# A first tap behind a copy on ScalarE, and block sums emitted over two plain tiles, in a two-layer encoder

## The chip, the cores and the metric

The kernel runs on one core of one Trainium2 chip. The metric is the time on the device in microseconds, the median of several runs. The core has five engines, each with a queue of instructions: TensorE (PE) multiplies matrices and writes into the banks of PSUM; VectorE (DVE) and ScalarE (ACT) do elementwise work; GpSimd (POOL) and SyncE (SP) mostly issue DMA transfers here. Engines wait for one another through semaphores.

## The reference

Two layers over 512 tokens of 1024 features, all in float32. Layer 0 mixes with an mLSTM and a memory attention, layer 1 with a band attention and a memory attention. After each mixer comes the same channel mixer, the part that the change is in:

```python
def conv_ffn(h, w_up, conv_w, conv_b, w_down):
    u, g = jnp.split(h @ w_up, 2, axis=-1)
    g = causal_dwconv(g, conv_w, conv_b)
    return (jax.nn.silu(g) * u) @ w_down
...
    x = x + jnp.concatenate([mix_out, mem_out], axis=-1) @ w_out
    x = x + conv_ffn(rmsnorm(x, norm_ffn_g[l]), ffn_w_up[l], ffn_conv_w[l], ffn_conv_b[l], ffn_w_down[l])
```

The hidden width is 2816, that is 22 tiles of 128 channels, each with an "up" and a "gate" half. The convolution has three taps along the tokens: y[t] = w2 g[t] + w1 g[t-1] + w0 g[t-2] + b.

## The kernel before

**Layout and precision.** Activations lie with the features on the 128 partitions and the 512 tokens along the free dimension: `xT` is 8 tiles of 128 x 512. A float32 operand is split into a high part (a cast, ScalarE, L142) and a low part (what is left, VectorE, L143), and `mm3` (L194 to L198) replaces one product by three matmuls: high x high, high x low, low x high. So every operand of a product costs one ScalarE and one VectorE instruction first. `scaled` (L329) does the same for an x tile times its norm gain (L331, L332).

**Stages of a layer.** Mixer; then `OutProjection.finish` (L710), which for each of the 8 x tiles takes the output projection's result (the last three x tiles, j = 5 to 7, are projected right there, 24 matmuls each), adds it to `xT[j]` (L715), sends `xT[j]` to DRAM, adds its square to the norm's sum (L290, L291) and makes the scaled high and low parts; then `channel_mixer` (L1014).

**The channel mixer.** The first three of the 22 tiles are *plain* (`PLAIN` = 3, `plain`, L759): gate and up are each a chain of 8 x 3 matmuls of 512 columns, then taps, Silu, products (L770 to L778) and the split of the result. The other 19 go through `step` (L874) with seven half-size products instead of eight. For that the x tiles are combined: `block_sums` (L781) is a generator; each of its four turns k takes x tiles k and k + 4, scales both on ScalarE (L787), forms four differences of 128 x 256 on VectorE (L796) and splits them (four casts on ScalarE, four low parts on VectorE). The weights are combined likewise by `Forms` (L916), one step ahead.

**One step.** TensorE runs seven chains of 12 matmuls of 256 columns. The first goes into bank r1, the second into r2; the third, fifth and sixth again into r1, the fourth and seventh into r3. Between the fifth and the sixth, and between the sixth and the seventh, stand chains of the down projection for tiles finished earlier: their number and length per step are given by `LOADS` and `UNITS` (L44 to L47), so that some steps have twice as much of it as others, and the last has none. ScalarE copies r1 out after the first chain (L890) and, through `sum_products` (L882), after the third, fifth and sixth; each next chain into r1 waits for the copy before it. VectorE adds r2 (L893).

**The tail.** What remains of a tile is done in the next step by a `Tail` (L980): `last_block` (L988, VectorE adds r3), `scaled` (L991, VectorE: gate times the norm row), `scaled_up` (L994, the same for up), `first_tap` (L996: on ScalarE, scale and bias, L750, and it prepares the other two taps), `second_tap` and `third_tap` (L743, VectorE; after the third ScalarE's Silu, L1006), `gated` (L1009), `split`. The first step of a layer has no tail. `split_fourth` (L970) splits the step's fourth weight sum: cast on ScalarE, low part on VectorE. `add_down` copies a down chain's result (L822) and adds it to x in DRAM with an accumulating DMA from the POOL queue (L823); the copies rotate through the `bias` buffers, four of them, of which the second layer holds two for the final gain.

**What sets the order.** Inside `later` (L850) a `manual_schedule` covers PE, ScalarE and VectorE: there each engine's queue is exactly the order in which the code emits. Everywhere else a planner orders each engine's queue by its own costs and due times: what is emitted earlier goes first, but an instruction whose inputs and buffers it takes to be ready may be put into a gap ahead of others. `weave(job, filler, each)` (L227) emits job and after each of its yields adds `each` to a counter; whenever that reaches 1, it emits one turn of the filler. The block sums are such a filler: one turn after each of the x tiles 4, 5 and 6 in `finish` (L719), the fourth turn in the first plain tile (five yields at 0.25).

**Buffers.** Split parts and block sums share the tag `u` (50 buffers of 128 x 512), temporaries the tag `t` (8), weights three pairs `wh`, `wl`, the step's weight halves `fh`, `fl` (4 each). PSUM: tag `mm` 3 banks, `sc` 3, `tr` 2.

Of the kernel before, what the change touches and what calls it, by code (L numbers as in the profile page):

```python
# [19 lines left out]
KT = D // P  # L20
# [36 lines left out]
def trunk(  # L57
# [34 lines left out]
    def sb(tag, shape, dtype=F32):  # L92
        count[0] += 1
        return pool.tile(shape, dtype, tag=tag, name=f"{tag}{count[0]}", bufs=bufs[tag])

    def ps(tag):
        count[0] += 1
        return psum.tile([P, S], F32, tag=tag, name=f"p{tag}{count[0]}", bufs=pbufs[tag])
# [101 lines left out]
    def project(w, c0, act, tag="mm"):  # L200


        n = len(act)
        wh, wl = weights(rows(w, c0, P), n, P)
        o = ps(tag)
        for k in range(n):
            mm3(o, wh[:, k, :], wl[:, k, :], act[k][0], act[k][1], k == 0, k == n - 1)
            yield
        return o

    def run(gen):
        while True:
            try:
                next(gen)
            except StopIteration as end:
                return end.value

    def chain(*gens):
        for g in gens:
            yield from g  # L220
# [6 lines left out]
    def weave(job, filler, each, lead=0):  # L227

        due = lead
        for n in chain([0], job):  # L230
            due += each if n is None else each * n
            while due >= 1:
                due -= 1
                next(filler, None)
# [39 lines left out]
    def logarithms():  # L274

        pin(A.preload_act_table_set("natural_log_exp_and_others"))

    class Norm:
# [14 lines left out]
        def finish(self):  # L293


            parts = [sb("t", [P, S], F32R) for _ in range(2)]
            split(*parts, self.acc)
            yield 7.4
            o = ps("sc")
            for i, part in enumerate(parts):  # L300
                nc.tensor.matmul(o, onesr, part, start=i == 0, stop=i == 1)
            v, r, t = sb("rb", [P, S]), sb("t", [P, S]), sb("t", [P, S])
            A.activation(t, o, AF.Ln, scale=1.0 / D, bias=eps)
            V.tensor_scalar(v, o, 1.0 / D, EPS, op0=ALU.mult, op1=ALU.add)
            A.activation(r, t, AF.Exp, scale=-0.5)
            A.activation(t, r, AF.Square)
            yield 4
            V.scalar_tensor_tensor(t, t, -0.5, v, op0=ALU.mult, op1=ALU.mult)
            self.row = sb("rb", [P, S])
            V.scalar_tensor_tensor(self.row, t, 1.5, r, op0=ALU.add, op1=ALU.mult)  # L310
# [18 lines left out]
    def scaled(t, g):  # L329
        hi, lo = sb("u", [P, S], F32R), sb("u", [P, S], F32R)  # L330
        A.activation(hi, t, AF.Copy, scale=g)  # L331
        V.scalar_tensor_tensor(lo, t, g, f(hi), op0=ALU.mult, op1=ALU.subtract)  # L332
        return hi, lo
# [121 lines left out]
    def reload_x():  # L455
        for j in range(KT):
            xT[j] = sb("fh" if j < KT // 2 else "fl", [P, S])
            tc.keep_in_program_order(nc.sync.dma_start(xT[j], xspill[j]))
# [6 lines left out]
    with tc.manual_schedule(engines={mybir.EngineType.PE, mybir.EngineType.Activation, mybir.EngineType.DVE}):  # L465
# [20 lines left out]
        def step(products, os_, k, order):  # L486
            for a, b in order:
                for i, o in enumerate(os_):
                    c = slice(i * P, (i + 1) * P)
                    st, mv = kv[k][a], memT[k][b]  # L490
                    first, last = (k, (a, b)) == (0, order[0]), (k, (a, b)) == (KT - 1, order[-1])
                    if products == "keys":
                        nc.tensor.matmul(o, st[:, c], mv, start=first, stop=last)
                    else:
                        nc.tensor.matmul(o, mv[:, c], st[:, MEM:], start=first, stop=last)
# [26 lines left out]
        for q in range(KT // 2):  # L522
            k = 2 * q
            step("keys", ko, k, weights_last if q else ((0, 0), (1, 0), (0, 1)))
            if not q:
                step("values", vo, k, weights_last)
            if q < KT // 2 - 1:
                split(*parts_of[q + 1], memory_rows(q + 1, ("tr", "sc")[q % 2], range(2)))
                for j in (k + 2, k + 3):
                    split(*kv[j], kvraw[j])  # L530
            if q:
                step("values", vo, k, weights_last)
            step("keys", ko, k + 1, weights_last)
            if q == KT // 2 - 1:
                kws1 = [parts(kraw1[0], block=0)]
                keep(0, 0, ko)
                kws1.append(parts(kraw1[1], block=1))
            step("values", vo, k + 1, weights_last)
# [151 lines left out]
    class OutProjection:  # L690
# [19 lines left out]
        def finish(self, mixer):  # L710
            logarithms()
            norm = mixer.norm
            for j in range(KT):
                o = self.o[j] if j in self.o else run(project(self.w, j * P, self.mixes))
                V.tensor_add(xT[j], xT[j], o)  # L715
                pin(G.dma_start(xspill[j], xT[j]))
                norm.add(xT[j])
                mixer.act.append(scaled(xT[j], mixer.gain[:, j : j + 1]))
                if KT // 2 <= j < KT - 1:  # L719
                    next(mixer.forms)  # L720

    class ChannelMixer:
# [151 lines left out]
        def step(self, j, w, nxt, tail):  # L874
            def then(o, *names):
                for name in names if o is not None else ():
                    getattr(o, name)()

            def sum_products(o, r, w, i):

                self.products(r, w, self.t(i))
                A.copy(o, r[:, :H])  # L882

            new = Tail(self, j)
            then(tail, "last_block", "scaled", "first_tap", "scaled_up")
            w.split_fourth()
            r1, r2, new.r3 = ps("mm"), ps("mm"), ps("sc")
            new.up, new.u3, new.pre = sb("t", [P, S]), sb("t", [P, S]), sb("t", [P, S])
            self.products(r1, w.a11, self.b(0, 0), True)
            A.copy(new.up[:, :H], r1[:, :H])  # L890
            then(tail, "second_tap", "third_tap")
            self.products(r2, w.a12, self.b(1, 0), True)
            V.tensor_tensor(out=new.up[:, :H], in0=new.up[:, :H], in1=r2[:, :H], op=ALU.add)  # L893
            sum_products(new.up[:, H:], r1, w.s2, 2)
            then(nxt, "sums")
            self.products(new.r3, w.s1, self.t(1), True)
            then(tail, "gated")
            then(nxt, "split_second", "sum_third")
            sum_products(new.u3[:, :H], r1, w.s3, 3)
            then(tail, "split")  # L900
            then(nxt, "split_up")
            V.tensor_tensor(out=new.pre[:, H:], in0=new.u3[:, :H], in1=new.r3[:, :H], op=ALU.add)
            w.down_products(0, 2)
            then(nxt, "split_sums", "sum_fourth")
            w.add_down(0)
            then(nxt, "split_gate")
            w.add_down(1)
            then(nxt, "split_down")
            sum_products(new.pre[:, :H], r1, w.a22, 4)
            w.down_products(2, 4)  # L910
            self.products(new.r3, w.s4, self.b(1, 1))
            w.add_down(2)
            w.add_down(3)
            return new, nxt
# [98 lines left out]

    def channel_mixer(mixer):  # L1014

        weave(mixer.plain(0), mixer.forms, 0.25)
        run(mixer.forms)
        mixer.buffers()
        skips = -(turn[0] + 2 * (PLAIN - 1)) % 3
        for j in range(1, PLAIN):  # L1020
            turn[0] += j <= skips
            run(mixer.plain(j))
        mixer.later()
        reload_x()
        return mixer.hid[FT - LAST :]
# [296 lines left out]
    mixer = ChannelMixer(0, col["gffn"][:, 0:8], more_rows)  # L1322
    outp.finish(mixer)
    hid = channel_mixer(mixer)
    logarithms()
    norm2, kvact, act = Norm(), [], []
# [134 lines left out]
    mixer = ChannelMixer(1, col["gffn"][:, 8:16], lambda: None)  # L1461
# [28 lines left out]
    def final_norm(T):  # L1490
# [8 lines left out]
        for c in range(0, S, step):  # L1499
# [5 lines left out]
            if last:  # L1505
                nc.scalar.dma_start(out[T * P : (T + 1) * P, :S], xt[T][0])

    hid = channel_mixer(mixer)
    n = LAST // 2
    for hf in range(2):  # L1510
# [76 lines left out]
```

## Time and profile before

| | |
|---|---|
| time, median of 3 runs | 1212.64 us (1211.23 to 1212.66) |
| the profiled execution's own time | 1212.91 us |
| its span, first to last instruction | 1211.2 us |
| mean granted TensorE clock | 0.997 |
| busy: VectorE, ScalarE | 986.1 us (81%), 741.4 us (61%) |
| HBM traffic over the span | 137 GB/s |

In the profile, a row of the timeline gives start and duration in us, engine, line of the kernel, operation, output and inputs, and in brackets the engine's idle time ahead of the instruction and what ended it. L142 and L143 are lines of a helper, so the tile names tell what is split: `fh`, `fl` a step's second, fourth or sixth weights, `wh`, `wl` other weights, `u` activations. A matmul that is shown with 0.28 us is pipelined: the next may start 0.11 us after it. The windows view gives the busy time of each engine in a stretch, the granted clock, and the DMA engines' share.

In the timeline the first layer's channel mixer covers about 280 to 597 us, the second's about 846 to 1166 us. The 38 copies at L890 lie between 310.6 and 1159.5 us.

### The profile page before, as it was taken

The numbers are of one execution on the slowest core, as the hardware profiler recorded it, in microseconds if no ns is written. First come the engines' busy times: TensorE is split into PE (matmuls) and PEld (weight loads), VectorE is DVE, ScalarE is ACT, GpSimd is POOL, SyncE is SP. The second block draws the span as 40 slices with busy tenths as digits, with TensorE's granted clock in tenths as the row PEclk, the third lists the DMA queues.
The fourth block names the chain that finished last, engine by engine and source line by source line (L and its number), as shares of the span: only waits on it lengthen the run. The fifth ranks groups of instructions, "written<-read, shape, count | busy, mean of one in ns | idle before, by whom it ended". The sixth has DMA issues, their size and how long they took to land.

```text
span 1211.2 us, 19132 instructions
## 1 busy us (share of the span) xinstructions
PE 1183.3 (98%) x7149; PEld 1044.9 (86%) x7149; DVE 986.1 (81%) x1768; ACT 741.4 (61%) x1345; POOL 143.1 (12%) x238
## 2 busy tenths in 40 slices
PE   9999999999999999999999999998998999999997
PEld 9988888887898899999888888787788889999986
DVE  6786788789789888888788888988977988888864
ACT  6448586667566555555566666767654655555545
POOL 1111101010122111011020001101011111011100
PEclk9999999999999999999999999999999999999999
DMA  8645324344677766655673323235447665656551
GB/s 286 213 108 140 80 76 128 92 147 116 150 164 155 164 161 161 140 139 114 175 216 85 89 60 125 77 105 163 133 99 139 131 140 139 140 139 140 122 156 70
DMA packets 200623, 162.87 MB, mean 134 GB/s; under 512 B 8680, under 2 KB 176334, under 8 KB 200530
## 3 DMA queue, kind: packets, MB, share of 16 engines
q1 hardware_dynamic: 182066, 119.74, 33.6%
q0 software_dynamic: 17888, 40.86, 18.0%
q8 instruction: 56, 0.92, 0.3%
q10 hardware_dynamic: 576, 1.05, 0.2%
q14 instruction: 37, 0.30, 0.1%
HBM read 128.89 MB, written 36.66 MB: 137 GB/s over the span
## 4 chain that ended last, share of the span: by engine, by line
PE 74%; issue 14%; DVE 6%; ACT 4%; DMA 2%; POOL 1%; POOLq 0%; SPq 0%; ACTq 0%; DVEq 0%
PE pmm L196 15%; PE pmm L197 14%; PE pmm L198 14%; PE ptr L197 5%; PE ptr L198 5%; PE ptr L196 5%; PE psc L198 4%; PE psc L197 4%; PE psc L196 3%; PE psc L602 2%; DVE wl L143 1%; ACT wh L142 1%; DMA wr<-in_a_w_in_dram 1%; ACT t L750 1%; PE ptr L1409 1%
## 5 line engine op out<-in xcount | busy, mean ns | idle before, releaser
L196 PE MATMUL pmm<-u,wh 128*128 128x512 f32 (+1 forms) x984 | 336.6, 342 | 0.2 <-ACT u L142 0.2
L198 PE MATMUL pmm<-u,wl 128*128 128x512 f32 (+1 forms) x984 | 332.1, 338 | 3.4 <-DVE wl L143 3.4
L197 PE MATMUL pmm<-u,wh 128*128 128x512 f32 (+1 forms) x984 | 332.2, 338 | 0.7 <-DVE u L332 0.7
L143 DVE TENSOR_TENSOR wl<-wr,wh 128x1024 fp32r<-128x1024 f32 (+4 forms) x172 | 195.4, 1137 | 82.2 <-ACT wh L142 81.7
L142 ACT CAST wh<-wr 128x1024 fp32r<-128x1024 f32 (+4 forms) x172 | 168.3, 981 | 83.3 <-PE pmm L197 33.2
L198 PEld LDWEIGHTS pmm<-u,wl 128*128 128x128 f32 x984 | 184.8, 188 | 23.3 <-DVE wl L143 4.0
L196 PEld LDWEIGHTS pmm<-u,wh 128*128 128x128 f32 x984 | 184.9, 188 | 18.6 <-ACT u L142 1.0
L197 PEld LDWEIGHTS pmm<-u,wh 128*128 128x128 f32 x984 | 185.0, 188 | 18.2 <-DVE u L332 1.4
L823 POOL DMA_DIRECT2D xspill<-bias x80 | 69.3, 874 | 445.2 <-ACT bias L822 417.9
L143 DVE TENSOR_TENSOR fl<-pt,fh 128x512 fp32r<-128x512 f32 x114 | 78.5, 689 | 36.7 <-ACT fh L142 33.8
L196 PE MATMUL ptr<-u,wh 128*128 128x512 f32 x272 | 106.4, 391 | 0.0
L197 PE MATMUL ptr<-u,wh 128*128 128x512 f32 x272 | 106.4, 391 | 0.0
L198 PE MATMUL ptr<-u,wl 128*128 128x512 f32 x272 | 106.0, 390 | 0.0
L196 PE MATMUL pmm<-u,fh 128*128 128x256 f32 x304 | 89.3, 294 | 13.6 <-ACT t L890 13.0
L142 ACT CAST fh<-pt 128x512 fp32r<-128x512 f32 x114 | 70.1, 617 | 26.2 <-DVE pt L939 26.0
L197 PE MATMUL pmm<-u,fh 128*128 128x256 f32 x304 | 85.3, 281 | 0.0
L198 PE MATMUL pmm<-u,fl 128*128 128x256 f32 x304 | 84.9, 279 | 0.0
L750 ACT ACTIVATE t<-t,cols 128x512 f32<-128x512 f32 x44 | 35.9, 816 | 71.3 <-DVE t L991 69.3
L196 PEld LDWEIGHTS pmm<-u,fh 128*128 128x128 f32 x304 | 57.6, 189 | 23.0 <-ACT t L890 20.9
L822 ACT COPY bias<-ptr 128x512 f32<-128x512 f32 x80 | 46.9, 589 | 41.1 <-PE ptr L198 35.5
L1006 ACT ACTIVATE t<-t 128x512 f32<-128x512 f32 x38 | 24.1, 633 | 74.9 <-DVE t L743 74.9
L198 PE MATMUL psc<-u,wl 128*128 128x256 f32 (+1 forms) x216 | 67.4, 312 | 0.4 <-DVE wl L143 0.4
(348 smaller groups left out, 2663.2 us busy)
## 6 DMA issues: line engine op xcount, KB each, us to landing
wr<-in_ffn_w_up_dram SPq DMA_DIRECT2D x50, 512.0 KB, 7.1
xspill<-bias POOLq DMA_DIRECT2D x80, 256.0 KB, 5.7
pt<-in_ffn_w_up_dram SPq DMA_DIRECT2D x38, 512.0 KB, 8.0
wr<-in_ffn_w_down_dram SPq DMA_DIRECT2D x34, 512.0 KB, 5.2
wr<-in_a_w_in_dram SPq DMA_DIRECT2D x20, 512.0 KB, 3.9
wr<-in_w_kv_dram SPq DMA_DIRECT2D x12, 512.0 KB, 3.9
xspill<-fh POOLq DMA_DIRECT2D x16, 256.0 KB, 2.6
xspill<-fl POOLq DMA_DIRECT2D x16, 256.0 KB, 2.5
```

Of the source, the lines that this page charges most:

```text
L142: high = A.copy(hi, src) if on_act else V.tensor_copy(hi, src)
L143: low = V.tensor_tensor(out=lo, in0=src, in1=f(hi), op=ALU.subtract)
L196: nc.tensor.matmul(o, lh, rh, start=first, stop=False, skip_group_check=more)
L197: nc.tensor.matmul(o, lh, rl, start=False, stop=False, skip_group_check=more)
L198: nc.tensor.matmul(o, ll, rh, start=False, stop=last, skip_group_check=more)
L602: nc.tensor.matmul(o, a, b, start=first and i == 0, stop=i == 1)
L750: A.activation(acc, src, AF.Identity, scale=self.fw[:, 2 * FT + j : 2 * FT + j + 1], bias=self.fb[:, j : j + 1])
L822: A.copy(t, o)
L823: G.dma_start(xspill[j], t, accum_op=ALU.add)
L1006: A.activation(self.acc, self.acc, AF.Silu)
L1409: nc.tensor.transpose(tp[:, b * P : (b + 1) * P], es[T, h][:, b * P : (b + 1) * P], ident)
```

## The change

Three edits:

- `OutProjection.finish` emits turns of the block sums only in layer 0. In layer 1 it emits none.
- `channel_mixer` weaves the block sums through all three plain tiles at 0.125 a yield, and emits what is left of them after the last plain tile instead of after the first. The first plain tile has five yields left after the norm, so no turn falls to it; each of the two others has 16 yields, so a turn follows its 8th yield (the end of its gate chain) and one its 16th (the end of its up chain). In layer 0 the fourth turn moves to the 8th yield of the second plain tile; in layer 1 all four turns are emitted in the second and third plain tile.
- In `step`, `first_tap` moves behind the first chain and its copy (L890), and `scaled_up` behind `split_fourth`. ScalarE's order at the start of a step was tap, cast, copy, and becomes cast, copy, tap. VectorE's was L988, L991, L994, low part, taps; it becomes L988, L991, low part, L994, taps.

```diff
@@ finish
-                if KT // 2 <= j < KT - 1:
+                if mixer.l == 0 and KT // 2 <= j < KT - 1:
                     next(mixer.forms)
@@ step
             new = Tail(self, j)
-            then(tail, "last_block", "scaled", "first_tap", "scaled_up")
+            then(tail, "last_block", "scaled")
             w.split_fourth()
+            then(tail, "scaled_up")
             r1, r2, new.r3 = ps("mm"), ps("mm"), ps("sc")
             new.up, new.u3, new.pre = sb("t", [P, S]), sb("t", [P, S]), sb("t", [P, S])
             self.products(r1, w.a11, self.b(0, 0), True)
             A.copy(new.up[:, :H], r1[:, :H])
-            then(tail, "second_tap", "third_tap")
+            then(tail, "first_tap", "second_tap", "third_tap")
@@ channel_mixer
-        weave(mixer.plain(0), mixer.forms, 0.25)
-        run(mixer.forms)
+        weave(mixer.plain(0), mixer.forms, 0.125)
         mixer.buffers()
         skips = -(turn[0] + 2 * (PLAIN - 1)) % 3
         for j in range(1, PLAIN):
             turn[0] += j <= skips
-            run(mixer.plain(j))
+            weave(mixer.plain(j), mixer.forms, 0.125)
+        run(mixer.forms)
         mixer.later()
```

## The prediction

> **What bounds the kernel now.** The page comes first, for the engine that is full.
>
> ```profile
> PE 1183.3 (98%) x7149; PEld 1044.9 (86%) x7149; DVE 986.1 (81%) x1768; ACT 741.4 (61%) x1345; POOL 143.1 (12%) x238
> ```
>
> TensorE is the bound, so an edit on ScalarE or VectorE pays only where TensorE waits for it. The view of waits, for TensorE (us in total, times, longest) and then for its weight loads, says where that is.
>
> ```profile
> PE pmm L196 <- ACT t L890: 13.0, 11, 3.1
> PE pmm L198 <- DVE wl L143: 3.4, 1, 3.4
> ...
> PE pmm L197 <- DVE u L332: 0.7, 2, 0.6
> ```
>
> ```profile
> PEld pmm L196 <- ACT t L890: 20.9, 37, 3.3
> ```
>
> L890 is ScalarE's copy of the first chain's result out of its bank in a seven-chain step; the third chain overwrites that bank and waits for the copy. 37 of the 38 steps wait, 11 of them so long that the matmuls themselves stand still. The two other rows are single stalls of up to 3.4 and 0.6 us, both ahead of the second layer's channel mixer, where the block sums run now. The two halves of the change touch these two places.
>
> **The tap moved behind the copy, in a long step.** One step with eight down chains, on ScalarE, VectorE and TensorE:
>
> ```profile
> 411.72 0.82 ACT L750 ACTIVATE t<-t,cols 128x512 f32<-128x512 f32 x1 [1.98 <-DVE t L991]
> 412.44 0.60 ACT L142 CAST fh<-pt 128x512 fp32r<-128x512 f32 x1
> 412.95 0.36 ACT L890 COPY t<-pmm 128x256 f32<-128x256 f32 x1
> 415.32 0.64 ACT L1006 ACTIVATE t<-t 128x512 f32<-128x512 f32 x1 [2.00 <-DVE t L743]
> 415.86 0.35 ACT L882 COPY t<-pmm 128x256 f32<-128x256 f32 x1
> ```
>
> ```profile
> 411.00 0.69 DVE L991 TENSOR_TENSOR t<-t,rb 128x512 f32<-128x512 f32 x1
> 411.60 0.69 DVE L994 TENSOR_TENSOR t<-t,rb 128x512 f32<-128x512 f32 x1
> 413.08 0.69 DVE L143 TENSOR_TENSOR fl<-pt,fh 128x512 fp32r<-128x512 f32 x1 [0.80 <-ACT fh L142]
> 413.69 1.53 DVE L743 SCALAR_TENSOR_TENSOR t<-t,cols,t 128x511 f32<-128x511 f32 x2
> ```
>
> ```profile
> 412.96 0.28 PE L197 MATMUL pmm<-u,wh 128*128 128x256 f32 x1
> 413.07 0.28 PE L198 MATMUL pmm<-u,wl 128*128 128x256 f32 x1
> 413.37 0.39 PE L196 MATMUL pmm<-u,fh 128*128 128x256 f32 x1
> 413.59 0.28 PE L197 MATMUL pmm<-u,fh 128*128 128x256 f32 x1
> ...
> 416.32 0.33 PE L196 MATMUL pmm<-u,wh 128*128 128x256 f32 x1
> ```
>
> Matmuls of 256 columns start 0.11 us apart (412.96, 413.07). The third chain starts at 413.37 instead of 413.18, and its second matmul comes 0.22 behind its first: 0.19 + 0.11 = 0.30 us lost, because L890 ends only at 413.31. Its data were there long before: the first chain's last matmul is twelve spacings ahead of 413.07, at 411.7, and takes 0.28, so they stand at 412.0. ScalarE was busy with the tap (0.82) and the cast (0.60).
>
> After: ScalarE idles 1.98 us before 411.72, so the cast goes there. The copy runs from 412.0 to 412.4, 0.8 before the third chain wants the bank, and the 0.30 is gone. The tap follows and ends at 412.4 + 0.82 = 413.2. On VectorE the cast's low half no longer waits 0.80; it goes at 411.6, L994 at 412.2, and VectorE is free at 412.8. So the two taps of L743 start at 413.24, still 0.45 earlier than now, though ScalarE's tap is later.
>
> What is late next: the fifth chain reuses the same bank and waits for L882, which on ScalarE stands behind Silu (L1006), behind the taps. It ends at 416.21 now and at 415.76 after; the fifth chain, at 416.32 now, will want to start 0.30 earlier, at 416.02. The new wait has 0.26 to spare. I take 0.30 for this kind of step. Of the 38 steps the first of each layer has no tail, and the edit doesn't touch it. That leaves 36; 11 are heavy, and 25 x 0.30 = 7.5 us.
>
> **The same, in a short step.** With four down chains TensorE comes round sooner and VectorE is late. VectorE and TensorE at such a boundary:
>
> ```profile
> 381.33 0.68 DVE L991 TENSOR_TENSOR t<-t,rb 128x512 f32<-128x512 f32 x1
> 381.93 0.68 DVE L994 TENSOR_TENSOR t<-t,rb 128x512 f32<-128x512 f32 x1
> 383.40 0.69 DVE L143 TENSOR_TENSOR fl<-pt,fh 128x512 fp32r<-128x512 f32 x1 [0.79 <-ACT fh L142]
> 384.01 0.75 DVE L743 SCALAR_TENSOR_TENSOR t<-t,cols,t 128x511 f32<-128x511 f32 x1
> ```
>
> ```profile
> 382.59 0.28 PE L198 MATMUL pmm<-u,wl 128*128 128x256 f32 x1
> 383.69 0.38 PE L196 MATMUL pmm<-u,fh 128*128 128x256 f32 x1 [0.82 <-ACT t L890]
> ```
>
> The third chain could start at 382.70 and starts at 383.69; with 0.11 for its second matmul, 1.1 us are lost. After, it starts on time, but VectorE decides what comes next: low half at 381.93, L994 at 382.53, taps at 383.13 instead of 384.01. ScalarE keeps up with that: first chain's last matmul twelve spacings before 382.59, its data at 381.5, copy until 381.9, tap after L991 until 382.9. Everything behind the taps, the fifth chain's release with it, is 0.88 earlier and not 1.1. So TensorE gains 0.88 and keeps some 0.2 as a wait of the fifth chain for L882. Of the 11 heavy waits nine are of this kind: 9 x 0.88 = 7.9 us.
>
> The two others are in the second layer, where ScalarE is held by a copy (L822) that waits for a DMA to free its buffer. ScalarE ahead of the worse one, TensorE at both, and two windows (length, then busy us of PE, PEld, DVE, ACT and POOL, granted clock, DMA share, GB/s):
>
> ```profile
> 915.47 0.59 ACT L822 COPY bias<-ptr 128x512 f32<-128x512 f32 x1 [3.61 <-DMA xspill<-bias]
> ```
>
> ```profile
> 898.97 0.39 PE L196 MATMUL pmm<-u,fh 128*128 128x256 f32 x1 [1.55 <-ACT t L890]
> ...
> 917.60 0.58 PE L196 MATMUL pmm<-u,fh 128*128 128x256 f32 x1 [3.09 <-ACT t L890]
> ```
>
> ```profile
> 917.20:920.60 3.40, 3.00 (x14) 3.00 (x15) 3.22 (x6) 1.01 (x4) 0.00 (x1) 0.50 0.91 174
> 838.00:842.00 4.00, 1.79 (x8) 1.47 (x9) 3.80 (x8) 3.10 (x7) 0.44 (x1) 1.00 0.25 90
> ```
>
> The DMA wait stays. Behind it the tap no longer stands ahead of cast and copy: the third chain goes 0.72 earlier (412.44 - 411.72, the tap's place in the queue), and the wait falls from 3.09 to about 2.4. The stretch behind it ran at clock 0.50 for 3.4 us, which cost half of it, 1.7; the 3.4 us stall near 840 left the clock at 1.00. So a wait of 3 us may or may not halve the clock; for 2.4 no row decides. Bounds: 0.7 if the clock falls again, 2.4 if not; I take the middle, 1.5, because the fifth chain waits for taps that are hardly earlier here. For the lighter of the two I take nothing, for the same reason.
>
> The Trainium skill, "TensorE: Matmul & The Clock Gate", Part 1 (the clock gate), says that the clock halves after an idle window of about 3.4 us, and that the windows run free of the kernel. The trace agrees loosely: a wait of 3.09 us was enough once, one of 3.4 was not. By the page 2.4 us would not be enough, this place would give 2.4, and the sum would be 0.9 more.
>
> **The block sums.** Nothing is added or removed; 4 sums a layer are emitted later. One sum's VectorE work is eight instructions like these four:
>
> ```profile
> 842.02 1.43 DVE L143 TENSOR_TENSOR u<-t,u 128x256 fp32r<-128x256 f32 x4
> ```
>
> 2 x 1.43 = 2.9 us at most, and two 512-wide scalings and four casts on ScalarE. In the second layer three sums are queued among the low halves (weights in L143, activations in L332) that TensorE waits for in those two stalls, and VectorE has no room there: 3.80 us busy of the 4.00 from 838. Without the sums ahead, 3.4 + 0.6 = 4.0 us go. The work must then fit elsewhere. The windows from the x tiles to the first step, with VectorE as the third busy time:
>
> ```profile
> 822.40:852.60 30.20, 26.27 (x113) 20.73 (x112) 28.98 (x54) 24.32 (x43) 4.34 (x8) 1.00 0.54 169
> 852.60:874.40 21.80, 21.80 (x98) 18.03 (x97) 20.34 (x32) 13.99 (x21) 0.00 (x0) 1.00 0.35 100
> 874.40:882.10 7.70, 7.70 (x47) 6.68 (x45) 6.80 (x10) 4.41 (x7) 0.00 (x0) 1.00 0.46 137
> ```
>
> 28.98 + 20.34 + 6.80 = 56.1 us of work; with 4.0 less there are 59.7 - 4.0 = 55.7 us. That is a tie, relieved by the last plain tile's end, which the first step's third chain doesn't need. It only works if the sums still run early, in gaps, though written later. Outside the hand-ordered part the planner does this:
>
> ```profile
> 865.95 0.69 DVE L939 TENSOR_TENSOR pt<-pt,wr 128x512 f32<-128x512 f32 x1 [0.74 <-DMA wr<-in_ffn_w_up_dram]
> 866.56 0.68 DVE L939 TENSOR_TENSOR pt<-wr,pt 128x512 f32<-128x512 f32 x1
> 867.16 0.68 DVE L775 TENSOR_TENSOR t<-t,rb 128x512 f32<-128x512 f32 x1
> ```
>
> L939 prepares the first step and is written after all plain tiles, yet it runs ahead of the first plain tile's own L775. I take the full 4.0. In the first layer only the fourth sum moves, by one plain tile, and no stall hangs on it: zero; without that slack, up to one sum, 2.9, would be late.
>
> **Sum.** 7.5 + 7.9 + 1.5 + 4.0 = 20.9 us. The profiled execution took 1212.91, 0.27 above the median of 1212.64; 1212.64 - 20.9 = 1191.7.
>
> **Rivals.**
>
> *The fifth chain's wait takes the place (slower).* The tap now waits for the first chain's copy, and Silu, L882 and the fifth chain queue behind it. If that line comes a further d later than I walked it, a long step gains nothing from d = 0.56 (0.26 + 0.30) and a short one from 0.88. With 5.5 from the other edits the kernel turns slower above 34 d = 25 x 0.56 + 7.9 + 5.5, d = 0.8. Were both VectorE instructions ahead of the taps pure delay, d = 1.2: 25 x 0.64 + 9 x 0.32 - 5.5 = +13, 1226. For it: 0.26 is little. Against it: VectorE's waits of 0.80 and 0.79, which vanish, pay for the order.
>
> *The sums run where they are written.* Three sums, 8.6 us, then leave the first window for the second: 20.34 + 8.6 is 7.1 more than 21.8, and the third window can take 0.9 of it. 6.2 lost against 4.0 regained, net 2.2 lost: 1212.64 - 16.9 + 2.2 = 1197.9. For it: VectorE is already full there. Against it: L939 above.
>
> *The copy does not get free.* The cast still stands ahead of it; if the cast waits for its source, the heavy waits stay: 7.5 + 4.0 remain, 1201.1. Against it: ScalarE's idle 1.98 before the tap.
>
> **How the numbers follow.** Forecast 0.66, sums in place 0.20, copy not free 0.08, fifth chain 0.06. Low end: all of 25 x 0.30, nine whole stalls of 1.1 (9.9), 2.4, the lighter DMA case's 1.55 and 4.0 give 25.4, so 1187; high end: just past the third rival, 1202. About 0.2%, 2.4 us, is what a measurement here can tell from no change. The first three cases are faster, less 0.02 for what none of them names: 0.92; slower 0.05; within 0.2% 0.03.
>
> **What would show it.** Right: the wait on L890 is nearly gone from TensorE's list, a small one on L882 appears in the nine short steps only, VectorE's low half no longer waits for its cast, the 3.4 us stall is gone, and no clock of 0.50 is granted late. Wrong: a wait on L882 in the long steps, or the third chain of the second layer's first step waiting for the sums' casts.

## The result and the profile after

The kernel after takes 1192.33 us (median of 4 runs, 1191.80 to 1192.85), the kernel before, timed beside it, 1211.93 us (1208.99 to 1212.66): a ratio of 0.9843, 95% interval 0.9825 to 0.9861. The profiled execution took 1192.76 us, 20.15 less than the profiled one of before, where 20.9 were forecast. From L883 on a line of the kernel before has a number one higher in the kernel after: the copy is L891, Silu L1007; L882, L750 and L743 stay.

The engines' busy time comes first, then TensorE's waits and one of its weight loads (us in total, times, longest).

```profile
PE 1171.5 (98%) x7149; PEld 1040.0 (87%) x7149; DVE 986.8 (83%) x1768; ACT 743.1 (62%) x1345; POOL 143.0 (12%) x238
```

```profile
PE pmm L196 <- ACT t L891: 6.3, 3, 4.3
PE pmm L196 <- ACT t L882: 2.0, 4, 0.7
```

```profile
PEld pmm L196 <- ACT t L882: 5.6, 13, 0.9
```

The instructions are as many as before. TensorE's busy time is 11.8 us shorter all the same, so more than waits has gone; the experiments come back to that. The copy of the first chain's result is waited for 3 times instead of 37. L882 is waited for 13 times: ahead of the fifth chain behind the nine boundaries that the prediction counts as short, as forecast, and behind the two that a DMA holds up, and ahead of the sixth chain of each layer's last step, where it was before too. The 3.4 us stall for the weights' low half is gone from the list. But one of the three waits that are left is 4.3 us long, and that is new. ScalarE and TensorE there, at the second layer's first step, and windows around it (length, then busy us of PE, PEld, DVE, ACT and POOL, granted clock, DMA share, GB/s):

```profile
867.55 0.70 ACT L787 ACTIVATE u<-fl,cols 128x512 f32<-128x512 f32 x1
...
870.25 1.00 ACT L142 CAST u<-t 128x256 fp32r<-128x256 f32 x3
871.16 0.36 ACT L891 COPY t<-pmm 128x256 f32<-128x256 f32 x1
```

```profile
866.98 0.28 PE L198 MATMUL pmm<-u,wl 128*128 128x256 f32 x1
871.57 0.58 PE L196 MATMUL pmm<-u,fh 128*128 128x256 f32 x1 [4.32 <-ACT t L891]
```

```profile
822.40:852.60 30.20, 30.20 (x135) 24.98 (x134) 25.32 (x36) 17.22 (x26) 1.62 (x3) 1.00 0.52 157
...
871.50:877.60 6.10, 6.03 (x28) 6.03 (x29) 5.34 (x12) 1.63 (x4) 0.00 (x0) 0.50 0.30 86
```

The fourth block sum is still being scaled at 867.55 and is cast at 870.25, and the first step's copy stands behind it in ScalarE's queue. TensorE starts nothing between 866.98 and 871.57, and then runs 6.1 us at half clock. The first window tells where the room went: until 852.6, where TensorE is now always busy, VectorE works 25.32 us, 3.7 fewer than before.

Where the 20 us come from can be read off the starts of the steps' third chains; the last row of each view is the sixth chain of the last step. Three rows of before and four of after:

```profile
584.02 0.39 PE L196 MATMUL pmm<-u,fh 128*128 128x256 f32 x1
...
882.12 0.38 PE L196 MATMUL pmm<-u,fh 128*128 128x256 f32 x1
...
1165.80 0.38 PE L196 MATMUL pmm<-u,fh 128*128 128x256 f32 x1
```

```profile
409.47 0.28 PE L196 MATMUL pmm<-u,fh 128*128 128x256 f32 x1
...
574.40 0.28 PE L196 MATMUL pmm<-u,fh 128*128 128x256 f32 x1
...
890.69 0.38 PE L196 MATMUL pmm<-u,fh 128*128 128x256 f32 x1 [1.00 <-ACT t L891]
...
1145.68 0.38 PE L196 MATMUL pmm<-u,fh 128*128 128x256 f32 x1
```

Eleven long steps lie between 413.37 and 584.02 before, 15.51 us each, and between 409.47 and 574.40 after, 14.99 each: 0.52 less a step, not 0.30. The second layer's first step starts its third chain at 882.12 before and 871.57 after, 10.55 ahead, and the second step's at 898.97 and 890.69, only 8.28 ahead: 2.3 are lost again, although the second step's own wait has become shorter (1.00 for 1.55). The first step ran at half clock, and that is the loss. The last steps' sixth chains (1165.80, 1145.68) are 20.12 apart.

### The profile page after: what moved, and what is told of

Read it like the earlier page. It is cut to its first block, busy times and chain, and to the rows that moved or that the text cites. A ratio compares the mean times of both kernels' runs of the same rounds, so it can differ in the third digit from the quotient of the medians.

```text
span 1191.0 us, 19097 instructions
## 1 busy us (share of the span) xinstructions
PE 1171.5 (98%) x7149; PEld 1040.0 (87%) x7149; DVE 986.8 (83%) x1768; ACT 743.1 (62%) x1345; POOL 143.0 (12%) x238
## 4 chain that ended last, share of the span: by engine, by line
PE 74%; issue 14%; DVE 7%; ACT 3%; POOL 1%; DMA 1%; POOLq 0%; ACTq 0%; DVEq 0%
PE pmm L196 15%; PE pmm L197 14%; PE pmm L198 14%; PE ptr L197 5%; PE ptr L198 5%; PE ptr L196 5%; PE psc L198 3%; PE psc L196 3%; PE psc L197 3%; PE psc L602 2%; DVE wl L143 1%; DVE t L743 1%; ACT wh L142 1%; DVE fl L143 1%; PE ptr L1410 1%
## 5 line engine op out<-in xcount | busy, mean ns | idle before, releaser
L196 PE MATMUL pmm<-u,fh 128*128 128x256 f32 x304 | 85.2, 280 | 6.3 <-ACT t L891 6.3
L197 PE MATMUL pmm<-u,fh 128*128 128x256 f32 x304 | 84.7, 279 | 0.0
L743 DVE SCALAR_TENSOR_TENSOR t<-t,cols,t 128x511 f32<-128x511 f32 x88 | 66.0, 750 | 10.4 <-ACT t L750 9.0
L196 PE MATMUL psc<-u,wh 128*128 128x256 f32 (+1 forms) x216 | 67.9, 314 | 0.3 <-ACT wh L142 0.3
L197 PE MATMUL psc<-u,wh 128*128 128x256 f32 (+1 forms) x216 | 67.5, 313 | 0.0
```

Source lines behind the costliest of these rows:

```text
L196: nc.tensor.matmul(o, lh, rh, start=first, stop=False, skip_group_check=more)
L197: nc.tensor.matmul(o, lh, rl, start=False, stop=False, skip_group_check=more)
L743: V.scalar_tensor_tensor(acc[:, n:], src[:, : S - n], self.fw[:, c * FT + j : c * FT + j + 1], acc[:, n:], op0=ALU.mult, op1=ALU.add,)
```

## The experiments

**One half of the change at a time.** The step's edit alone (its two `then` lines, with the block sums as in the kernel before) and the sums' edit alone (the step as before):

```diff
@@ step's edit alone
-            then(tail, "last_block", "scaled", "first_tap", "scaled_up")
+            then(tail, "last_block", "scaled")
             w.split_fourth()
+            then(tail, "scaled_up")
...
-            then(tail, "second_tap", "third_tap")
+            then(tail, "first_tap", "second_tap", "third_tap")
```

> The kernel before with the step's edit alone (first tap behind the copy, L994 behind the cast). My reading of the two traces: the tap's edit gave about 23 us (0.53 in a long step, about 1 in a short one) and the block sums' edit took about 3 back (2.3 between the second layer's x tiles and the end of its first step, about 0.9 ahead of the first layer's first step), so about 1189, 3 below the changed kernel. The prediction as it stands on record: the tap gave 16.9 and the sums 4.0, so about 1196, 4 above it.

> The kernel before with the block sums' edit alone. My reading: the first step of the second layer waits some 4 us for ScalarE behind the last sums' casts and then runs at half clock for some us, against 4.7 us of stalls removed: 1214 to 1216. The prediction on record: 1208, no such wait.

The step's edit alone took 1189.43 us (4 runs, 1188.96 to 1190.97; before beside it 1211.14), ratio 0.9818 (0.9803 to 0.9832). The sums' edit alone took 1213.5 us (10 runs, 1212.10 to 1215.39), ratio 1.0019 (1.0009 to 1.0029), a little under the range expected. So the step's edit brings 21.7 us and the sums' edit loses 2.4; together that is 19.3, and both at once brought 19.6. TensorE's waits with the step's edit alone, then with the sums' edit alone:

```profile
PE pmm L198 <- DVE wl L143: 3.4, 1, 3.4
PE pmm L196 <- ACT t L891: 2.3, 2, 1.5
```

```profile
PE pmm L196 <- ACT t L890: 16.6, 12, 4.4
```

The 3.4 us stall goes with the sums' edit and the 4.4 us one comes with it, whatever the step does. The split into 21.7 and 2.4 has an uncertainty that the medians don't show: in the trace of the step's edit alone TensorE ran at half clock behind the 3.4 us stall, where the profile of the kernel before has 1.00 (the window from 838 in the prediction).

```profile
830.20:833.30 3.10, 3.10 (x9) 2.31 (x9) 3.10 (x8) 2.73 (x6) 0.00 (x0) 0.50 0.55 163
```

That is half of 3.1, some 1.6 us, which one kernel pays in its profiled run and the other doesn't.

**The third chain in a bank of its own.** This asks what a long step loses to the copy at all, with ScalarE's and VectorE's order left as in the kernel before. The third chain goes into a bank of its own and no longer adds to the first chain's result, so "up" lacks a part of its sum, and so do the fifth and sixth chain. The fifth chain, too, no longer waits for the copy of the third's result.

```diff
+            r4 = ps("mm")
...
-            sum_products(new.up[:, H:], r1, w.s2, 2)
+            sum_products(new.up[:, H:], r4, w.s2, 2, True)
```

> The kernel before, but the third chain goes into a PSUM bank of its own instead of adding onto the first chain's; the first chain's part is then missing from that quarter of up, and the third's from the sums behind it. ScalarE's and VectorE's order is that of before. If TensorE's stop itself is what slows the 256-column matmuls behind it (0.119 instead of 0.113 us apart until the down chain), a long step takes 15.0 us and all chains run at 0.113. If ScalarE's and VectorE's work beside them does it, chains three to five stay at 0.119 and a long step takes 15.2.

It took 1188.1 us (one run), and its long steps 14.99 us, as in the kernel after. Now the spacing of matmuls, since it is there that busy time has gone. The fourth chain's first and last of 12, in the kernel before, after, and in this one:

```profile
414.89 0.28 PE L196 MATMUL psc<-u,wh 128*128 128x256 f32 x1
...
416.20 0.28 PE L198 MATMUL psc<-u,wl 128*128 128x256 f32 x1
...
417.74 0.40 PE L196 MATMUL ptr<-u,wh 128*128 128x512 f32 x1
```

```profile
424.58 0.28 PE L197 MATMUL pmm<-u,fh 128*128 128x256 f32 x1
...
425.82 0.28 PE L196 MATMUL psc<-u,wh 128*128 128x256 f32 x1
...
427.07 0.28 PE L198 MATMUL psc<-u,wl 128*128 128x256 f32 x1
...
428.54 0.40 PE L196 MATMUL ptr<-u,wh 128*128 128x512 f32 x1
```

```profile
424.44 0.28 PE L196 MATMUL psc<-u,wh 128*128 128x256 f32 x1
...
425.68 0.28 PE L198 MATMUL psc<-u,wl 128*128 128x256 f32 x1
```

Before, 1.31 us for 11 spacings, 0.119 each; after, 1.25 or 0.114; here 1.24 or 0.113. From the third chain's second matmul to the down chain it is 417.74 - 413.59 = 4.15 before and 428.54 - 424.58 = 3.96 after. So a stop costs 0.29 where it stands (0.52 from 413.07 to 413.59, where two spacings would be 0.23) and 0.19 more in the matmuls behind it, 0.48 of the 0.52 measured. That the engines' other order isn't what spaces the matmuls wider is shown by this kernel, which keeps the order of before and runs at 0.113. That the stop itself does it is what is left; the trace doesn't show how.

**Which move frees the copy.** This experiment and the next start from the version with the second layer's sums in the first plain tile, which is told below (1186.86 us). In this one the cast goes first, but the tap stays ahead of the copy.

```diff
-            then(tail, "scaled_up")
+            then(tail, "first_tap", "scaled_up")
...
-            then(tail, "first_tap", "second_tap", "third_tap")
+            then(tail, "second_tap", "third_tap")
```

> The version with the sums in the first plain tile (1186.9 us), with ScalarE's order cast, tap, copy in place of cast, copy, tap. Theory A, what pays is that the cast leaves the queue ahead of the copy and goes into ScalarE's idle time: the long steps keep their 0.53 us, the nine short ones wait 0.35 to 0.5 us for the copy again, about 1190 us. Theory B, what pays is that the copy stands ahead of the tap: TensorE stops in all 34 steps as in the kernel before, about 1206 us (1186.9 + 25 x 0.53 + some 6 from the short steps).

1191.99 us (4 runs, 1190.34 to 1194.20), ratio to before 0.9836 (0.9809 to 0.9862), 5.1 more than its base and 2 more than Theory A's 1190. The profiled execution is the slowest of the four, 1194.20. ScalarE in a long step:

```profile
422.78 0.82 ACT L750 ACTIVATE t<-t,cols 128x512 f32<-128x512 f32 x1 [1.46 <-DVE t L992]
423.50 0.35 ACT L891 COPY t<-pmm 128x256 f32<-128x256 f32 x1
```

The copy ends at 423.85 and the third chain, due at 424.24, starts on time: the long steps keep their 14.99 us. What pays in a long step is the cast's move into ScalarE's idle time; the tap's place doesn't matter there. It matters in the short steps, which wait again (up to 0.82 us), and most in the two steps of the second layer that a DMA holds up:

```profile
887.15 0.49 PE L196 MATMUL pmm<-u,fh 128*128 128x256 f32 x1 [2.70 <-ACT t L891]
...
907.17 0.39 PE L196 MATMUL pmm<-u,fh 128*128 128x256 f32 x1 [3.00 <-ACT t L891]
```

```profile
888.00:889.00 1.00, 1.00 (x7) 1.00 (x6) 0.96 (x3) 0.01 (x1) 0.00 (x0) 0.50 1.13 216
...
909.00:910.00 1.00, 1.00 (x6) 1.00 (x6) 0.96 (x3) 0.95 (x2) 0.00 (x0) 0.50 0.52 100
```

These are waits of 2.70 and 3.00 us, and the clock is at 0.50 behind both.

**The tap later by a known time.** Two more copies on ScalarE between the first chain's copy and the tap, which test the slower rival.

```diff
             A.copy(new.up[:, :H], r1[:, :H])
+            for _ in range(2 if tail is not None else 0):
+                A.copy(new.u3[:, :H], new.up[:, :H])
```

> The version with the sums in the first plain tile (1186.9 us), with two further ScalarE copies of 128x256 between the copy of the first chain's result and the tap, in each step that has a tail: the tap, Silu and the copy of the third chain's result come some 0.54 us later, d of the prediction's first rival. If the fifth chain hangs on the taps as the prediction said, with 0.26 us to spare in a long step: 25 x 0.28 + 9 x 0.54 = 12 us more, about 1199; if the 0.2 us of slower matmuls behind each stop come as well in the long steps, 25 x 0.5 + 9 x 0.54 = 17, about 1204. If the taps are early enough for the fifth chain whatever they wait for: no change, 1187.

1212.59 us (10 runs, 1211.45 to 1212.92), ratio to before 1.0002 (0.9990 to 1.0013): the whole gain is gone, 8.6 us above the highest of the expected figures. TensorE's waits, ScalarE in a long step, and TensorE at its fifth chain:

```profile
PE pmm L196 <- ACT t L882: 19.9, 36, 1.2
```

```profile
424.57 0.37 ACT L891 COPY t<-pmm 128x256 f32<-128x256 f32 x1 [1.76 <-PE pmm L198]
424.98 0.84 ACT L893 COPY t<-t 128x256 f32<-128x256 f32 x2
425.73 0.81 ACT L750 ACTIVATE t<-t,cols 128x512 f32<-128x512 f32 x1
...
428.74 0.35 ACT L882 COPY t<-pmm 128x256 f32<-128x256 f32 x1
```

```profile
428.34 0.28 PE L198 MATMUL psc<-u,wl 128*128 128x256 f32 x1
429.15 0.38 PE L196 MATMUL pmm<-u,wh 128*128 128x256 f32 x1 [0.53 <-ACT t L882]
```

The expectation's d of 0.54 was too small: the two copies between SBUF tiles take 0.84 us, and the tap starts 1.16 behind the copy (424.57 to 425.73). In the kernel after that is 0.27, and the end of the line is:

```profile
423.30 0.37 ACT L891 COPY t<-pmm 128x256 f32<-128x256 f32 x1 [1.76 <-PE pmm L198]
423.57 0.82 ACT L750 ACTIVATE t<-t,cols 128x512 f32<-128x512 f32 x1
...
426.59 0.35 ACT L882 COPY t<-pmm 128x256 f32<-128x256 f32 x1
```

So d = 0.89. With the extra copies the fifth chain starts 0.06 behind the end of L882 (428.74 + 0.35 = 429.09). In the kernel after L882 ends at 426.94 and the chain starts at 427.18, 0.11 behind the 427.07 above, so 0.18 are to spare. 0.89 - 0.18 = 0.71; the chain comes at 429.15 instead of 428.45, 0.70 late. A long step takes 15.83 us, 0.84 more than in the kernel after: the 0.70, and again a slower restart behind the stop. The rival's mechanism is right, and its line holds by less than 0.2 us.

**The sums elsewhere.** In the second layer all four sums in the last five yields of the first plain tile; the first layer's sums as in the kernel before, the step as in the kernel after:

```diff
-        weave(mixer.plain(0), mixer.forms, 0.125)
+        weave(mixer.plain(0), mixer.forms, 0.8 if mixer.l else 0.25)
+        run(mixer.forms)
...
-            weave(mixer.plain(j), mixer.forms, 0.125)
-        run(mixer.forms)
+            run(mixer.plain(j))
```

> The step's edit, and in the second layer no sums at the x tiles but all four emitted within the first plain tile's last five yields, ahead of its result's split; first layer as before. If the sums run where they are emitted, because their buffers are handed out in that order, they end some 20 us ahead of the first step: no wait of 4 us there, no half clock, and the x tiles' stalls of 3.4 and 0.6 stay away: about 1185. If VectorE has no room wherever they stand, a stall of 2 to 4 us comes in a plain tile instead: 1188 to 1190.

1186.86 us (4 runs, 1186.71 to 1187.79), ratio 0.9796 (0.9781 to 0.9810). That is between the two expected cases. Neither the 3.4 us stall nor the 4.3 us one is there, and at the second layer's first step it is 4.3 us ahead of the kernel with the step's edit alone, 1.6 of them by the half clock shown above. In the medians 2.6 are left of it (1189.43 to 1186.86), less than the prediction's 4.0: the first step's third chain waits 0.97 us here, and the second's 1.60 instead of 0.79.

Then the same in the first layer too, its rate also 0.8 and no sums at its x tiles:

> The version with the sums in the first plain tile (1186.9 us), with the first layer's four sums put there too, none at its x tiles. If they find VectorE idle there as in the second layer: 1185 to 1187 us. If the first layer's plain tiles leave VectorE less room: one sum of 2.9 us or more is late, 1188 to 1191 us.

1189.24 us (4 runs, 1187.93 to 1189.67), ratio 0.9810 (0.9788 to 0.9832), in the second case of the expectation and 2.4 more than with the second layer alone. The intervals of the two ratios overlap, but the trace has stops of 0.67, 0.36 and 0.37 us in the first layer's plain tiles, where the other has 0.16 and 0.40, so there the x tiles look like the better place.

Then the kernel after with its sums where it writes them, but with their buffers taken at the x tiles, which asks why the planner puts them so late:

```diff
+                if mixer.l == 1 and KT // 2 <= j < KT - 1:
+                    mixer.reserve()
...
+        def reserve(self):
+            held = [sb("u", [P, S]), sb("u", [P, S]), sb("t", [P, S]), sb("t", [P, S])]
+            held += [sb("u", [P, S], F32R) for _ in range(4)]
+            for t in held:
+                G.memset(f(t)[:, :1], 0.0)
+            self.held.append(held)
```

The sums then take their buffers from `held`.

> The kernel after, with one addition in the second layer: at each of the fifth, sixth and seventh x tiles the buffers of one block sum are taken and one column of each is set by a short GpSimd instruction (24 in all); the sums themselves are written where the kernel after writes them. Theory A, the order in which buffers of one name are handed out is what keeps the sums late: the three sums now run in VectorE's idle time ahead of the plain tiles' product, the 4.3 us wait of the third chain in the second layer's first step and the 6.1 us at half clock behind it go, 1186 to 1189 us. Theory B, VectorE is simply full between the x tiles and the first step: the wait stays, 1191 to 1193 us.

1184.32 us (4 runs, 1183.38 to 1185.92), ratio to before 0.9773 (0.9746 to 0.9800), better than Theory A's range, and 5.1 below the step's edit alone. A sum's first instruction on VectorE, the third chain of the second layer's first step, and two windows:

```profile
829.35 0.41 DVE L806 TENSOR_TENSOR t<-u 128x256 f32<-128x256 f32 x1
```

```profile
865.85 0.28 PE L196 MATMUL pmm<-u,fh 128*128 128x256 f32 x1
```

```profile
822.40:852.60 30.20, 30.20 (x135) 24.98 (x134) 30.11 (x54) 23.29 (x41) 2.30 (x19) 1.00 0.46 138
...
867.00:875.00 8.00, 8.00 (x57) 7.34 (x56) 7.05 (x12) 4.75 (x8) 1.68 (x2) 1.00 0.32 72
```

L806 is the sums' line here. The first sum runs at 829.35, 21.5 us ahead of its place in the kernel after (850.85), VectorE is full until 852.6, the chain isn't held up and the clock stays at 1.00. Theory A holds: the order of the sums' code is unchanged, and only their buffers are taken earlier. So the planner does fill gaps with what is written later, but not ahead of the moment at which the buffers come free. Which instruction holds them isn't shown; that it is one of the first plain tile fits. In the kernel after, the first sum follows directly on the cast that ends the first plain tile:

```profile
848.98 0.61 ACT L142 CAST u<-t 128x512 fp32r<-128x512 f32 x1
849.50 0.72 ACT L787 ACTIVATE u<-fh,cols 128x512 f32<-128x512 f32 x1
```

**The first layer's fourth sum.** The kernel after stops once ahead of the first layer's first step where the kernel before does not:

```profile
299.23 0.50 PE L196 MATMUL psc<-u,wh 128*128 128x512 f32 x1 [0.34 <-ACT wh L142]
```

The last version puts that sum back into the first plain tile and keeps the buffers taken early; the kernel after ran beside it once more.

```diff
-        weave(mixer.plain(0), mixer.forms, 0.125)
+        weave(mixer.plain(0), mixer.forms, 0.125 if mixer.l else 0.25)
```

> The version with the buffers taken at the x tiles (1184.3 us), with the first layer's fourth sum back in the first plain tile, as in the kernel before. Every traced kernel with that sum in the second plain tile takes 32.2 us from its last norm product (280 us) to the third chain of the first layer's first step, every one with it in the first plain tile 31.4, with a TensorE wait for a weight's cast in the one and not in the other. Theory A, the sum's new place is what holds that cast up: 31.4 here too, and 1183.5 us. Theory B, it comes from another part of the change, as the planner's order shifts: 32.2 stays, 1184.3 us.

> The kernel after itself, in the same call as the version above, so that the two stand side by side: 1192 us, and 32.2 us for the stretch ahead of the first layer's first step.

1183.73 us (4 runs, 1182.66 to 1184.08), ratio to before 0.9764 (0.9749 to 0.9779), the best of all, and 1191.65 us for the kernel after (5 runs, 1190.76 to 1192.95; 0.9834, 0.9818 to 0.9850). From the first layer's last norm product to the first step's third chain the new version takes 31.4 us (279.11 to 310.54), as the kernel before does (280.12 to 311.52); the kernel after takes 32.3 (280.25 to 312.50, and 279.95 to 312.25 in the second run). Theory A holds in the trace: the sum's new place costs 0.8 us. In the medians, 0.6 apart and measured at different times, it can't be told from nothing. One kernel doesn't fit the expectation's "every one": with all four sums in the first plain tile, and stops of its own, the stretch takes 33.5.

## Why the prediction came out nearly right

The total (20.9 forecast, 20.15 measured in the profiled executions, 19.6 in the medians) is closer than its terms. For the step's edit 16.9 were forecast and 21.7 measured, for the sums' edit 4.0 gained and 2.4 lost. That two errors of opposite sign nearly cancel is luck.

**The long step: right in mechanism, its size 0.30 for 0.52.** The cast goes into the idle time, the low half no longer waits for it, the copy is early, the third chain follows at 0.11. The step that failed is "0.19 + 0.11 = 0.30 us lost": it counted the stop and took the matmuls behind it as unchanged, though the rows it stood on have them (from 413.59 to 416.32 are 23 spacings, 0.119 each). In 22 undisturbed steps of this kind that is 11.4 us for 6.6. One sentence there is wrong besides: the third chain does not overwrite the first chain's bank, it adds to it. The wait is the same, for a sum may not grow before the copy has read it. And what the prediction counts as eight and four down chains are eight and four products of three matmuls each; between the fifth and the sixth chain of a long step stand 24 matmuls in two chains.

**The short step: right.** VectorE and TensorE after:

```profile
379.98 0.69 DVE L143 TENSOR_TENSOR fl<-pt,fh 128x512 fp32r<-128x512 f32 x1
...
381.18 1.53 DVE L743 SCALAR_TENSOR_TENSOR t<-t,cols,t 128x511 f32<-128x511 f32 x2
```

```profile
383.38 0.28 PE L198 MATMUL psc<-u,wl 128*128 128x256 f32 x1
383.75 0.39 PE L196 MATMUL pmm<-u,wh 128*128 128x256 f32 x1
```

VectorE's low half has no wait ahead of it now, nor have its taps, and the fifth chain comes 0.37 behind the fourth's end instead of 0.11: the 0.2 that TensorE was to keep as a wait. Such steps take 12.7 us from third chain to third chain, 0.8 to 0.95 less than the 13.6 before; 0.88 was forecast. At two of the nine boundaries, those where the third chain waited 1.36 us, the step behind is a long one and the fifth chain waits 0.66 us in its place: 1.44 are gained ahead of them and 0.46 lost again behind.

**The DMA-held steps: too little.** 1.5 were forecast, with a wait of 2.4 us and the half clock open. The waits are 1.00 (890.69 above) and 1.02 us, and no half clock follows. From third chain to third chain the stretch ahead of the worse one is 1.5 us shorter, and the one behind it 1.7, in which a short step's gain is contained. The DMA itself holds ScalarE 2.41 us at the worse one, where it was 3.61, so the copy gains from that too. All steps outside the 22 long ones and the second layer's first give 12.1 us, from the first layer's first third chain and the second layer's second to the sixth chain of each layer's last step, where 10.3 were forecast (7.9 + 1.5 + 3 x 0.30).

**The block sums: wrong.** 4.0 were forecast and 2.4 us lost. The step that failed is "It only works if the sums still run early, in gaps, though written later", with L939 as its evidence. L939 writes a buffer that the plain tiles don't use (`pt`); the sums share `u` and `t` with them. The rival that the sums run where they are written is what happened in the second layer, and its net 2.2 is close, but not by its working: VectorE was not too full, it had time left before 852.6 (25.32 us busy of 30.20). The new wait of 4.3 us cancels what went (10.65 ahead at the first layer's last sixth chain, 10.55 at the second layer's first step), and the half clock behind it is the loss. The sign that the prediction gave for being wrong, the third chain of that step behind the sums' casts, is exactly the row at 871.57. In the first layer the term set at zero is a loss of 0.8 us, the stop at 299.23 with the slower restart behind it; on ScalarE the moved sum's scalings and casts (from 292.31 to 296.76 us) stand ahead of the weights' casts that TensorE waits for.

**The rivals.** The slower one didn't happen, and the run with two extra copies shows that it was real: its line has 0.18 us to spare (0.26 was forecast), and at d = 0.89 the gain is gone, where the prediction put the turn at 0.8. The copy that doesn't get free is refuted by the list of waits.

## What to carry to other kernels

Before reordering a queue, look for the instruction in front that could have run in the engine's idle time: here the cast, not the tap, held the copy in the long steps. Price a short stall by the time until the engine is back at its pace, not by the gap alone. When work is emitted later in the hope that a planner fills gaps with it, see which buffers it takes and who has to let go of them first; buffers taken early left the order of the code as it was and brought 8.0 us more (1192.33 to 1184.32).

## What the hardware showed

Matmuls of 256 columns that follow a stop of 0.3 us run 0.119 us apart instead of 0.114, through the rest of that chain and two more, up to the next chain of 512 columns; without the stop they don't.

The clock was halved behind TensorE's waits of 2.70, 3.00, 3.09, 4.31, 4.32 and 4.42 us. Behind the stall of 3.35 us (3.4 in the lists), at the same place in three kernels, it was halved in two, the step's edit alone and the third chain in its own bank, and not in the kernel before. No wait of up to 2.05 us halved it in any of the twelve traces, and none lies between 2.05 and 2.70. So for the 2.4 us that the prediction asked about no run decides. How long the half clock lasts varies between runs of one kernel: behind the 4.32 us wait of the kernel after it was 6.1 us, in the second run, behind a wait of 4.31, some 3:

```profile
871.20:874.30 3.10, 3.06 (x15) 3.06 (x16) 3.10 (x8) 0.72 (x2) 0.00 (x0) 0.52 0.00 0
874.40:877.40 3.00, 3.00 (x26) 2.91 (x25) 2.23 (x5) 1.09 (x4) 0.00 (x0) 1.00 0.62 180
```

The Trainium skill, "TensorE: Matmul & The Clock Gate", Part 1, has it that the clock halves after an idle window of about 3.4 us, and that the windows run free. The traces agree in that the same wait at the same place halved the clock in one run and not in another. They differ in that waits of 2.70, 3.00 and 3.09 us, shorter than that window, halved it here; the measurement decides.
